# Unread products on the array, alternating input and weights, and key norms moved into the next block: two layers of a hybrid encoder on one Trainium2 core

## The chip, the core and the metric

The kernel runs on one core of a Trainium2 (trn2) chip. The metric is device time in microseconds (us) of one execution of the program; lower is better. The program is one launch that reads all its inputs and weights from HBM and writes the result there.

## What is computed

Two layers of an encoder trunk over x of 256 positions by 1024 features, in float32 throughout. Cut to what matters here:

```python
def reference(x, mem, ...):
    h = x
    for l in range(2):
        hn = rms_norm(h, norm_mix[l])
        if l == 0:
            z = hn @ hy_w_in                          # 1024 x (1824 RWKV columns + 512 S5 columns)
            y_a = rwkv7_time_mix(z[..., :1824], ...)  # 8 heads of 64, a recurrence over time
            y_b = s5_ssm(z[..., 1824:], ...)          # diagonal complex scan, 32 groups
            y_mix = concatenate([y_a, y_b]) @ hy_w_out
        else:
            y_mix = diff_attention(hn, ...)
        h = h + y_mix
        h = h + memory_cross_attention(rms_norm(h, norm_xattn[l]), rms_norm(mem, norm_mem[l]), ...)
        hn = rms_norm(h, norm_ffn[l])
        y_ff = swiglu(hn, ...) if l == 0 else moe_swiglu(hn, ...)   # 8 experts, top 2
        h = h + y_ff
    return h

def memory_cross_attention(h, mem_n, w_q, w_kv, q_gain, k_gain, w_o):
    k, v = split(mem_n @ w_kv, 2)                     # 256 x 1024 each
    k = rms_norm(k.reshape(1, 256, 4, 256), k_gain)   # a norm per head
    ...
```

The memory keys and values depend on `mem` and on the weights alone, not on h, so they can be computed at any time before the attention that reads them.

## The kernel before, in words

**Products.** Activations stand feature-major, in 8 blocks of 128 features by 256 positions. A float32 matrix product is done in three products of a reduced type: each operand is split in a high part (`xh`, `wh`) and a rest (`xl`, `wl`), and `mm3` (L188 to L192) issues high by high, high by rest, rest by high. The generator `chunks` (L164) loads two blocks of weights (512 KB) by a DMA on SP into a `raw` buffer (L173), lets ACT make `wh` by a copy (L178) and DVE `wl` by a subtraction (L184). `weight_pools(cx, raw, split, per)` sets how many raw and split buffers there are; in the stages of layer 0 in question `(3, 2, 2)`: three raw buffers.

**Start.** The input x (1 MB) is loaded in four DMAs on SP (L251), then the constants (L252); ACT and DVE split it in `xh` (L257) and `xl` (L258). `first_factor` (L261 to L280) squares x on ACT (L265), adds on POOL (L267), sums over features on the array, takes the power −1/2 and spreads the norm's factor over the partitions by a product with a diagonal matrix (`dg`, L278) into `rsB0`. The u-projection (the 512 S5 columns) runs through `feat_linear` meanwhile, in PSUM tiles `pm`, and `uT` (L300) is its result times `rsB0`. Then come the other input columns, first those of `hy_m`.

**Chain and filler.** The RWKV recurrence and the S5 scan of layer 0 are a long chain of small array products (32x32 and 32-row ones: `pbu`, `py`, `pm<-w,aa`, `pm<-qq,vt`) with DVE, POOL and ACT between. Beside them the kernel computes the memory keys and values of both layers, `memory_kv(l)` (L478 to L516), as filler for the array: four blocks n per layer (n = 0, 1 keys, n = 2, 3 values), each two PSUM tiles `pf` of 128 x 512, accumulated over 8 blocks of weights split by ACT and DVE (`fwh` L450, `fwl` L453). The function is a generator: every `yield` gives a cost and returns to a pipeline that puts pieces of chain and of filler in turn, and a scheduler then sets the order on every engine.

After a key block the norm stands between it and the next block: ACT squares `pf` straight from PSUM (L499), POOL makes the power −1/2 (`rsqrt_small`, L200 and L201), ACT scales from PSUM into `kx` (L504), the array transposes `kx` (`ptf`, L508, in a tile of the same PSUM pool as `pf`), ACT multiplies by the gain (L512), and a DMA on POOL's queue stores it (L515).

```python
            for b in range(2):
                kx = fs2.tile([128, 512], F32, name="kx", tag="kx")
                if n >= 2:
                    nc.scalar.activation(kx, p[b], AF.Copy)
                    nc.gpsimd.dma_start(vdr[l][2 * b + n - 2], kx)
```

**Router.** In front of the experts of layer 1 the array makes the logits (`lgp`) and transposes the tokens (`pt`, L1646); then `choose()` takes the two largest on DVE (L1688 to L1694, the last writes `sel`), and the array's next work is the ranks `rkp` from `sel`. After it the experts' products (`pgt`, `pgu`, `pd`) read 352 MB of weights; SP loads each MB as a buffer comes free (L1808).

Of the kernel before, what the change touches and what calls it, by code (L numbers as in the profile page):

```python
# [18 lines left out]
EPS = 1e-6  # L19
# [37 lines left out]
KX = 1  # L57
# [66 lines left out]
def kernel(ctx: ExitStack, tc: tile.TileContext, a: dict, out: bass.AP, dbg=None):  # L124
# [104 lines left out]
    fs2 = scoped(cright, "fs2", 2, side="right")  # L229
# [20 lines left out]
    for c in range(0, 8, X0C):  # L250
        nc.sync.dma_start(x0[:, c:c + X0C], a["xT"][:, c:c + X0C])  # L251
    nc.sync.dma_start(cst, a["consts"])  # L252
    one = sp.tile([128, 128], F32, name="one")
    nc.gpsimd.memset(one, 1.0)
    for c in range(8):
        g = col("gn0", c)
        nc.scalar.activation(xt[0][:, c], x0[:, c], AF.Copy, scale=g)  # L257
        nc.vector.scalar_tensor_tensor(xt[1][:, c], x0[:, c], g, xt[0][:, c], op0=ALU.mult, op1=ALU.subtract)  # L258
# [24 lines left out]
    first_factor()  # L283
# [14 lines left out]
    feat_linear(a["hy"][3], [(p[m // 2][:, m % 2], m * 128, 128, m % 2 == 0) for m in range(4)])  # L298
# [178 lines left out]
    def memory_kv(l):  # L477
# [3 lines left out]
        nc.gpsimd.tensor_tensor(gg, cols[:, lo:hi], cols[:, lo2:hi2], op=ALU.mult)  # L481
        for n in range(4):
            p = [ps_fl.tile([128, 512], F32, name="pf", tag="fl") for b in range(2)]
            for k, wh, wl in fchunks(a["wkv"][4 * l + n], 8, f"gm{l}"):
                for b in range(2):
                    t = slice(b * 128, (b + 1) * 128)
                    mm3(p[b], (mth[:, k, t], mtl[:, k, t]), (wh, wl), k == 0, k == 7)
                    yield 0.65
            for b in range(2):
                kx = fs2.tile([128, 512], F32, name="kx", tag="kx")  # L490
                if n >= 2:
                    nc.scalar.activation(kx, p[b], AF.Copy)
                    nc.gpsimd.dma_start(vdr[l][2 * b + n - 2], kx)
                    yield 0.0
                    continue
                ss = smf.tile([128, 2], F32, name="ssk", tag="ss2")
                for j in range(2):
                    js = slice(j * 256, j * 256 + 256)
                    nc.scalar.activation(kx[:, js], p[b][:, js], AF.Square, accum_out=ss[:, j:j + 1])  # L499
                rs = smf.tile([128, 2], F32, name="rsk", tag="ss2")  # L500
                rsqrt_small(rs, ss, 2, 1.0 / 256, EPS, smf)
                for j in range(2):
                    js = slice(j * 256, j * 256 + 256)
                    nc.scalar.activation(kx[:, js], p[b][:, js], AF.Copy, scale=rs[:, j:j + 1])  # L504
                yield 0.0
                pt = ps_fl.tile([128, 2, 2, 128], F32, name="ptf", tag="fl")
                for c in range(4):
# [1711 lines left out]
```

## Time and profile before

| what | value |
|---|---|
| median of 3 runs | 1676.42 us (1673.38 to 1678.52) |
| the profiled execution: its time | 1677.01 us |
| the profiled execution: span of the trace | 1675.1 us |
| PE (TensorE) busy | 1606.2 us, 96% |
| DVE (VectorE), ACT (ScalarE), POOL (GpSimd) busy | 645.6, 480.1, 207.4 us |
| mean granted clock of TensorE | 0.975 |

The profiled execution's time is 1.9 us longer than its span, and 0.6 us above the median. Busy time counts instructions that run; PE is the matmuls, PEld the weight loads that go beside them. The granted clock is given as a share of full speed; a stretch shows either 1.00 (2.4 GHz) or 0.50 (1.2 GHz). "Idle before <- releaser" says how long an engine stood in front of an instruction, and whose work ended that.

### The profile page before, as it was taken

The numbers are of one execution on the slowest core, as the hardware profiler recorded it, in microseconds if no ns is written. First come the engines' busy times: TensorE is split into PE (matmuls) and PEld (weight loads), VectorE is DVE, ScalarE is ACT, GpSimd is POOL, SyncE is SP. The second block draws the span as 40 slices with busy tenths as digits, with TensorE's granted clock in tenths as the row PEclk, the third lists the DMA queues.
The fourth block names the chain that finished last, engine by engine and source line by source line (L and its number), as shares of the span: only waits on it lengthen the run. The fifth ranks groups of instructions, "written<-read, shape, count | busy, mean of one in ns | idle before, by whom it ended". The sixth has DMA issues, their size and how long they took to land. (4 is left out here: it accounts for less than half of the span.)

```text
span 1675.1 us, 34301 instructions
## 1 busy us (share of the span) xinstructions
PE 1606.2 (96%) x14830; PEld 977.4 (58%) x14830; DVE 645.6 (39%) x1081; ACT 480.1 (29%) x861; POOL 207.4 (12%) x256
## 2 busy tenths in 40 slices
PE   5999999999999999998999999999999899999997
PEld 5867657899999988898324333343333323333432
DVE  7778987676555567764201011100101001011011
ACT  6465434554544456653101000010000100010000
POOL 6334473121000032111000000000000000000000
PEclk9999979999999999999899999999999999999998
DMA  6423323564555543645789889999999999999895
GB/s 224 153 89 126 105 75 113 221 257 150 181 195 173 187 147 127 251 139 201 301 354 399 335 363 405 404 419 418 418 419 418 419 419 418 418 419 392 346 419 238
DMA packets 74464, 471.50 MB, mean 281 GB/s; under 512 B 8600, under 2 KB 10008, under 8 KB 22464
## 3 DMA queue, kind: packets, MB, share of 16 engines
q1 hardware_dynamic: 73024, 465.02, 71.5%
q0 software_dynamic: 1280, 4.20, 0.7%
q8 instruction: 118, 1.93, 0.5%
q14 instruction: 42, 0.34, 0.1%
HBM read 463.94 MB, written 5.24 MB: 280 GB/s over the span
## 5 line engine op out<-in xcount | busy, mean ns | idle before, releaser
L195 PE MATMUL pgu<-raw,gx 128*32 128x512 f32 (+1 forms) x5376 | 520.5, 544 | 5.7 <-DMA raw<-mg 3.3
L195 PEld LDWEIGHTS pgu<-raw,gx 128*32 128x32 f32 x5376 | 171.4, 111 | 330.8 <-issue 290.0
L195 PE MATMUL pd<-raw,th 128*32 128x512 f32 x2352 | 262.7, 597 | 0.4 <-DVE th L1908 0.4
L184 DVE TENSOR_TENSOR wl<-raw,wh 128x1024 fp32r<-128x1024 f32 (+1 forms) x159 | 194.0, 1232 | 105.2 <-ACT wh L178 104.9
L178 ACT ACTIVATE wh<-raw 128x1024 fp32r<-128x1024 f32 (+1 forms) x160 | 165.6, 1047 | 149.2 <-PE pgu L191 69.2
L1894 DVE SCALAR_TENSOR_TENSOR actA<-pgu,gs,actA 128x512 f32<-128x512 f32 (+1 forms) x32 | 21.9, 684 | 481.2 <-ACT actA L1890 272.6
L195 PEld LDWEIGHTS pd<-raw,th 128*32 128x32 f32 x2352 | 76.4, 111 | 174.9 <-issue 171.8
L190 PE MATMUL pm<-xh,wh 128*128 128x256 f32 (+1 forms) x552 | 161.1, 295 | 15.2 <-ACT wh L178 13.3
L192 PE MATMUL pm<-xh,wl 128*128 128x256 f32 (+1 forms) x552 | 157.9, 290 | 5.3 <-DVE wl L184 5.3
L191 PE MATMUL pm<-xl,wh 128*128 128x256 f32 (+1 forms) x552 | 158.6, 289 | 2.1 <-DVE xl L1096 2.1
L1890 ACT ACTIVATE actA<-pgu,gs 128x512 f32<-128x512 f32 (+1 forms) x32 | 20.3, 635 | 444.8 <-PE pgu L195 444.7
L190 PEld LDWEIGHTS pm<-xh,wh 128*128 128x128 f32 (+1 forms) x552 | 106.7, 194 | 18.4 <-ACT wh L178 13.8
L192 PEld LDWEIGHTS pm<-xh,wl 128*128 128x128 f32 (+1 forms) x552 | 106.1, 194 | 7.4 <-DVE wl L184 6.6
L191 PEld LDWEIGHTS pm<-xl,wh 128*128 128x128 f32 (+1 forms) x552 | 107.1, 194 | 3.6 <-DVE xl L1096 2.5
L191 PE MATMUL pgu<-xl,wh 128*128 128x256 f32 x352 | 99.3, 282 | 0.0
L190 PE MATMUL pgu<-xh,wh 128*128 128x256 f32 x352 | 99.2, 282 | 0.0
L192 PE MATMUL pgu<-xh,wl 128*128 128x256 f32 x352 | 99.1, 282 | 0.0
L1833 POOL CAST mv<-cst 128x256 fp32r<-128x256 f32 x8 | 3.6, 448 | 650.9 <-PE ptp L195 626.0
L192 PEld LDWEIGHTS pgu<-xh,wl 128*128 128x128 f32 x352 | 66.4, 189 | 0.0
L191 PEld LDWEIGHTS pgu<-xl,wh 128*128 128x128 f32 x352 | 66.3, 188 | 0.0
L190 PEld LDWEIGHTS pgu<-xh,wh 128*128 128x128 f32 x352 | 66.2, 188 | 0.0
L453 DVE SCALAR_TENSOR_TENSOR fwl<-fraw,cols,fwh 128x512 fp32r<-128x512 f32 x64 | 56.1, 885 | 11.6 <-ACT fwh L450 11.6
(482 smaller groups left out, 2182.3 us busy)
## 6 DMA issues: line engine op xcount, KB each, us to landing
raw<-mg SPq DMA_DIRECT2D x112, 1024.0 KB, 19.1
raw<-mu SPq DMA_DIRECT2D x112, 1024.0 KB, 17.9
raw<-md SPq DMA_DIRECT2D x112, 1024.0 KB, 18.7
raw<-wgu SPq DMA_DIRECT2D x22, 1024.0 KB, 4.9
fraw<-wkv SPq DMA_DIRECT2D x32, 512.0 KB, 3.8
raw<-wqkv SPq DMA_DIRECT2D x12, 1024.0 KB, 4.9
raw<-wdn SPq DMA_DIRECT2D x11, 1024.0 KB, 4.8
raw<-hy SPq DMA_DIRECT2D x16, 512.0 KB, 3.9
```

The source lines that it names most:

```text
L178: W["act"].append(nc.scalar.activation(wh, rv, AF.Copy).ins)
L184: W["dve"].append(e_.tensor_tensor(wl[:, c_], rv[:, c_], wh[:, c_], op=ALU.subtract).ins)
L190: nc.tensor.matmul(out, lhsT=lt[0], rhs=r[0], start=start, stop=False, **kw)
L191: nc.tensor.matmul(out, lhsT=lt[0], rhs=r[1], start=False, stop=False, **kw)
L192: nc.tensor.matmul(out, lhsT=lt[1], rhs=r[0], start=False, stop=stop, **kw)
L195: nc.tensor.matmul(out, lhsT=lt, rhs=r, start=start, stop=stop, **kw)
L453: e_.scalar_tensor_tensor(wl, rv, g, wh, op0=ALU.mult, op1=ALU.subtract)
L1833: nc.gpsimd.tensor_copy(mv[:, :, 0:128], ident[:, None, :].to_broadcast([128, 2, 128]))
L1890: nc.scalar.activation(actA, p[0], AF.Silu, scale=gs[:, 0, 1:2])
L1894: nc.vector.scalar_tensor_tensor(actA, p[1], gs[:, 0, 1:2], actA, op0=ALU.mult, op1=ALU.mult)
```

## The change

Five edits:

1. `awake(p, n, x)` issues n products of a 128x128 float32 tile with itself into a PSUM tile that nothing reads. 24 stand at the very start (of the tile `one`, all ones), 12 after the router's logits and tokens (of the identity).
2. `entry()` loads x in four pairs of blocks and alternates each pair with the u-projection's weight loads on SP, and the splits likewise on ACT and DVE; the constants are loaded, and `first_factor` issued, after the u-projection's products.
3. In `memory_kv` each block is copied from PSUM to `kx` by one ACT operation. The key norm is a generator of its own, `keys()`, which works from SBUF, puts its transposes in the PSUM pool `ps_tr`, and is run after k = 2 and k = 4 of the next block's products.
4. The pool `fs2`, which holds `kx` and `kx2`, has three buffers instead of two.
5. The `weight_pools` of the stage that reads `w_glu` and `hy_out` has two raw buffers instead of three.

```diff
--- before.py
+++ after.py
@@ -226,7 +226,7 @@
     fkp = scoped(cright, "fkp", 1, side="right")
     frw = scoped(cright, "frw", 2, side="right")
     fwp = scoped(cright, "fwp", 3, side="right")
-    fs2 = scoped(cright, "fs2", 2, side="right")
+    fs2 = scoped(cright, "fs2", 3, side="right")
     smf = scoped(cright, "smf", 2, side="right")
     cx = ExitStack()
     s5t = scoped(cx, "s5t", 2)
@@ -247,15 +247,15 @@
     x0 = sp.tile([128, 8, T], F32, name="x0")
     nc.sync.dma_start(cols, a["cols"])
     xt = new_xt(xtp1)
-    for c in range(0, 8, X0C):
-        nc.sync.dma_start(x0[:, c:c + X0C], a["xT"][:, c:c + X0C])
-    nc.sync.dma_start(cst, a["consts"])
     one = sp.tile([128, 128], F32, name="one")
     nc.gpsimd.memset(one, 1.0)
-    for c in range(8):
-        g = col("gn0", c)
-        nc.scalar.activation(xt[0][:, c], x0[:, c], AF.Copy, scale=g)
-        nc.vector.scalar_tensor_tensor(xt[1][:, c], x0[:, c], g, xt[0][:, c], op0=ALU.mult, op1=ALU.subtract)
+
+    def awake(p, n, x):
+
+        for _ in range(n):
+            nc.tensor.matmul(p[:, 0:128], lhsT=x, rhs=x, start=True, stop=True, skip_group_check=True)
+
+    awake(ps_fl.tile([128, 128], F32, name="awake", tag="fl"), 24, one)
     rsB0 = rp.tile([128, T], F32, name="rsB0")
 
     def first_factor():
@@ -280,7 +280,7 @@
         nc.scalar.activation(rsB0, p, AF.Copy)
 
     gts, gstt, gtt = nc.gpsimd.tensor_scalar, nc.vector.scalar_tensor_tensor, nc.gpsimd.tensor_tensor
-    first_factor()
+
     def feat_linear(src, groups, cw=512):
 
         for k, wh, wl in chunks(src, 8, cw):
@@ -295,7 +295,28 @@
     yb = uT
 
     p = [ps_mm.tile([128, 2, T], F32, name="pm", tag="mm") for _ in range(2)]
-    feat_linear(a["hy"][3], [(p[m // 2][:, m % 2], m * 128, 128, m % 2 == 0) for m in range(4)])
+
+    def entry():
+
+        for c in range(0, 8, 2):
+            nc.sync.dma_start(x0[:, c:c + 2], a["xT"][:, c:c + 2])
+            for e in (c, c + 1):
+                g = col("gn0", e)
+                nc.scalar.activation(xt[0][:, e], x0[:, e], AF.Copy, scale=g)
+                nc.vector.scalar_tensor_tensor(xt[1][:, e], x0[:, e], g, xt[0][:, e], op0=ALU.mult, op1=ALU.subtract)
+            yield
+
+    pairs, w8 = entry(), chunks(a["hy"][3], 8, 512)
+    for k in range(8):
+        if k % 2 == 0:
+            next(pairs)
+        _, wh, wl = next(w8)
+        for m in range(4):
+            ms = slice(m * 128, m * 128 + 128)
+            mm3(p[m // 2][:, m % 2], (wh[:, ms], wl[:, ms]), (xt[0][:, k], xt[1][:, k]),
+                k == 0 and m % 2 == 0, k == 7, skip_group_check=True)
+    nc.sync.dma_start(cst, a["consts"])
+    first_factor()
     for m2 in range(2):
         nc.vector.tensor_tensor(uT[:, 2 * m2:2 * m2 + 2], p[m2], rsb(2), op=ALU.mult)
     hcst = hk.tile([128, NHCONST], F32, name="hcst")
@@ -479,6 +500,7 @@
         lo, hi = COLS[f"gq{l}"]
         lo2, hi2 = COLS[f"gk{l}"]
         nc.gpsimd.tensor_tensor(gg, cols[:, lo:hi], cols[:, lo2:hi2], op=ALU.mult)
+        late = []
         for n in range(4):
             p = [ps_fl.tile([128, 512], F32, name="pf", tag="fl") for b in range(2)]
             for k, wh, wl in fchunks(a["wkv"][4 * l + n], 8, f"gm{l}"):
@@ -486,34 +508,36 @@
                     t = slice(b * 128, (b + 1) * 128)
                     mm3(p[b], (mth[:, k, t], mtl[:, k, t]), (wh, wl), k == 0, k == 7)
                     yield 0.65
+                if k in (2, 4) and late:
+                    yield from late.pop(0)
             for b in range(2):
                 kx = fs2.tile([128, 512], F32, name="kx", tag="kx")
+                nc.scalar.activation(kx, p[b], AF.Copy)
                 if n >= 2:
-                    nc.scalar.activation(kx, p[b], AF.Copy)
                     nc.gpsimd.dma_start(vdr[l][2 * b + n - 2], kx)
-                    yield 0.0
-                    continue
-                ss = smf.tile([128, 2], F32, name="ssk", tag="ss2")
-                for j in range(2):
-                    js = slice(j * 256, j * 256 + 256)
-                    nc.scalar.activation(kx[:, js], p[b][:, js], AF.Square, accum_out=ss[:, j:j + 1])
-                rs = smf.tile([128, 2], F32, name="rsk", tag="ss2")
-                rsqrt_small(rs, ss, 2, 1.0 / 256, EPS, smf)
-                for j in range(2):
-                    js = slice(j * 256, j * 256 + 256)
-                    nc.scalar.activation(kx[:, js], p[b][:, js], AF.Copy, scale=rs[:, j:j + 1])
+                else:
+                    late.append(keys(l, gg, n, b, kx))
                 yield 0.0
-                pt = ps_fl.tile([128, 2, 2, 128], F32, name="ptf", tag="fl")
-                for c in range(4):
-                    nc.tensor.transpose(pt[:, c // 2, c % 2], kx[:, c * 128:(c + 1) * 128], ident)
-                kx2 = fs2.tile([128, 2, 2, 128], F32, name="kx2", tag="kx")
-                for e in range(2):
-                    if KX:
-                        nc.scalar.activation(kx2[:, :, e], pt[:, :, e], AF.Copy, scale=gg[:, e:e + 1])
-                    else:
-                        nc.vector.tensor_scalar(kx2[:, :, e], pt[:, :, e], gg[:, e:e + 1], None, op0=ALU.mult)
-                nc.gpsimd.dma_start(kdr[l][2 * n + b], kx2.rearrange("p a b c -> p (a b c)"))
-                yield 0.45
+
+    def keys(l, gg, n, b, kx):
+
+        ss = smf.tile([128, 2], F32, name="ssk", tag="ss2")
+        kx2 = fs2.tile([128, 2, 2, 128], F32, name="kx2", tag="kx")
+        for j in range(2):
+            nc.scalar.activation(kx2[:, j].rearrange(f2), kx[:, j * 256:j * 256 + 256], AF.Square, accum_out=ss[:, j:j + 1])
+        rs = smf.tile([128, 2], F32, name="rsk", tag="ss2")
+        rsqrt_small(rs, ss, 2, 1.0 / 256, EPS, smf)
+        for j in range(2):
+            js = slice(j * 256, j * 256 + 256)
+            nc.scalar.activation(kx[:, js], kx[:, js], AF.Copy, scale=rs[:, j:j + 1])
+        yield 0.0
+        pt = ps_tr.tile([128, 2, 2, 128], F32, name="ptf", tag="tr")
+        for c in range(4):
+            nc.tensor.transpose(pt[:, c // 2, c % 2], kx[:, c * 128:(c + 1) * 128], ident)
+        for e in range(2):
+            nc.scalar.activation(kx2[:, :, e], pt[:, :, e], AF.Copy, scale=gg[:, e:e + 1])
+        nc.gpsimd.dma_start(kdr[l][2 * n + b], kx2.rearrange("p a b c -> p (a b c)"))
+        yield 0.45
 
     low_priority(lambda: behind(MAT, memory_norm), LPM)
     cs_.close()
@@ -752,7 +776,7 @@
     ps_bm = scoped(cx, "ps_bm", 3, space=PSUM)
     ps_po = scoped(cx, "ps_po", 1, space=PSUM)
     ub = scoped(cx, "ub", 2)
-    weight_pools(cx, 3, 2, 2)
+    weight_pools(cx, 2, 2, 2)
     rs2 = scoped(cx, "rs2", 2)
     u1 = scoped(cx, "u1", 1)
 
@@ -1719,6 +1743,7 @@
                 tokens(j - 2)
         for f in TORD:
             (logits if f > 0 else tokens)(abs(f))
+        awake(ps_mm.tile([128, 128], F32, name="awake", tag="mm"), 12, ident)
     hv = hT.rearrange("p (j b) t -> p b j t", b=2)
 
     choose()
```

The new order on each engine, at three places. First ACT at the start, before the change (`x_122` is the input, `ac`, `sq` its squares, `s5t`, `s5c`, `tbl` the S5 tables):

```order
L257 ACT_TABLE_LOAD
L257 ACTIVATE xh<-x_122,cols 128x256 x2
L265 ACTIVATE ac_150<-x_122 128x512
L257 ACTIVATE xh<-x_122,cols 128x256 x2
L265 ACTIVATE sq_151<-x_122 128x512
L257 ACTIVATE xh<-x_122,cols 128x256 x4
L265 ACTIVATE sq_151<-x_122 128x512
L178 ACTIVATE wh<-raw 128x1024 x2
```

and with it:

```order
L305 ACT_TABLE_LOAD
L305 ACTIVATE xh<-x_122,cols 128x256 x2
L265 ACTIVATE ac_298<-x_122 128x512
L178 ACTIVATE wh<-raw 128x1024
L305 ACTIVATE xh<-x_122,cols 128x256 x2
L265 ACTIVATE sq_299<-x_122 128x512
L178 ACTIVATE wh<-raw 128x1024
L355 ACTIVATE s5t_335<-cols 128x16
L305 ACTIVATE xh<-x_122,cols 128x256 x2
L265 ACTIVATE sq_299<-x_122 128x512
```

The first weight split moves from behind all eight splits of x and three squares to behind two splits and one square.

PE in the recurrence of layer 0, where the keys of layer 1's block n = 0 are normed, before:

```order
L195 MATMUL pbu<-uT,sbw 128x256 x2
L195 MATMUL pm<-w,aa 32x32 x17
L195 MATMUL py<-xc,cpad 32x256
L195 MATMUL pm<-w,aa 32x32 x20
L195 MATMUL py<-xc,cpad 32x256
L195 MATMUL pm<-w,aa 32x32 x27
L195 MATMUL pm<-qq,vt 32x32 x21
L508 MATMUL ptf<-cst,kx 128x128 x4
L195 MATMUL pm<-qq,vt 32x32 x11
```

and with the change, at the same block's transposes:

```order
L190 MATMUL pf<-fwh,mth 128x512
L191 MATMUL pf<-fwl,mth 128x512
L192 MATMUL pf<-fwh,mtl 128x512
L195 MATMUL pm<-qq,vt 32x32
L190 MATMUL pf<-fwh,mth 128x512
L195 MATMUL pm<-qq,vt 32x32 x4
L536 MATMUL ptf<-cst,kx 128x128 x4
L195 MATMUL pm<-qq,vt 32x32 x27
L191 MATMUL pf<-fwl,mth 128x512
L192 MATMUL pf<-fwh,mtl 128x512
```

No `pf` product stood between the small products before; now those of the next block do, and the transposes stand among them.

PE at the router, before:

```order
L195 MATMUL lgp<-ones,sqr 128x1 x4
L1646 MATMUL pt<-cst,hT 128x128 x4
L195 MATMUL rkp<-sel,mcst 128x16
L195 MATMUL rkp<-sel,ones 128x8
```

and with the change:

```order
L1670 MATMUL pt<-cst,hT 128x128 x4
L256 MATMUL awake<-cst 128x128 x12
L195 MATMUL rkp<-sel,mcst 128x16
L195 MATMUL rkp<-sel,ones 128x8
```

The twelve unread products stand where the array waited for `sel`.

## Rows read from the trace of the kernel before

**Rows 1.** Cores: span and mean granted clock.
```profile
core 0: 1675.1 us, clock 0.975
```

**Rows 2.** Windows: stretch, us; busy of PE, PEld, DVE, ACT, POOL; clock; DMA; GB/s.
```profile
0.00:36.60 36.60, 18.72 (x116) 17.71 (x117) 25.01 (x60) 25.76 (x46) 24.13 (x48) 0.91 0.70 230
...
225.60:242.70 17.10, 16.71 (x291) 10.28 (x292) 15.38 (x25) 6.54 (x17) 13.44 (x17) 0.50 0.06 20
...
263.10:300.00 36.90, 36.90 (x266) 29.68 (x265) 22.98 (x46) 17.42 (x37) 8.45 (x12) 1.00 0.41 140
```

**Rows 3.** Waits of PE, 0 to 42 us: total, times, longest.
```profile
PE pm L190 <- ACT wh L178: 13.3, 2, 11.7
```

**Rows 4.** Timeline of PE: start, length, what, [idle before <- releaser].
```profile
11.73 0.58 PE L190 MATMUL pm<-xh,wh 128*128 128x256 f32 x1 [11.73 <-ACT wh L178]
...
17.41 0.28 PE L190 MATMUL pm<-xh,wh 128*128 128x256 f32 x1
```

**Rows 5.** Timeline of ACT at the start.
```profile
5.87 0.91 ACT L257 ACTIVATE xh<-x,cols 128x256 fp32r<-128x256 f32 x2
...
10.64 2.10 ACT L178 ACTIVATE wh<-raw 128x1024 fp32r<-128x1024 f32 x2
...
18.93 3.30 ACT L412 ACTIVATE tbl<-cst,s5c 128x256 f32<-128x256 f32 x8 [4.92 <-POOL s5c L345]
...
33.41 0.36 ACT L280 ACTIVATE rsB<-ssp 128x256 f32<-128x256 f32 x1
```

**Rows 6.** Timeline of DVE: the result of the u-projection.
```profile
35.62 1.28 DVE L300 TENSOR_TENSOR uT<-pm,rsB 128x512 f32<-128x512 f32 x2
```

**Rows 7.** Timeline of PE in the recurrence, around the key norm.
```profile
219.72 1.26 PE L195 MATMUL pm<-qq,vt 32*32 32x32 f32 x122
...
223.44 1.13 PE L195 MATMUL pbu<-uT,sbw 32*128 32x256 f32 x4 [0.88 <-DVE zz L562]
...
225.99 1.06 PE L195 MATMUL py<-xc,cpad 128*32 128x256 f32 x2 [1.00 <-POOL xc L575]
...
228.66 0.91 PE L195 MATMUL pm<-w,aa 32*32 32x32 f32 x51
...
230.10 1.11 PE L508 MATMUL ptf<-cst,kx 128*128 128x128 f32 x4
...
238.82 0.78 PE L190 MATMUL pf<-fwh,mth 128*128 128x512 f32 x1
```

**Rows 8.** Timeline of ACT, that norm: first square, scaling.
```profile
221.91 0.39 ACT L499 ACTIVATE kx<-pf 128x256 f32<-128x256 f32 x1 [3.70 <-PE pf L192]
...
228.81 0.84 ACT L504 ACTIVATE kx<-pf,rsk 128x256 f32<-128x256 f32 x2 [5.46 <-POOL rsk L201]
```

**Rows 9.** Timeline of PE at the router.
```profile
790.24 1.09 PE L1646 MATMUL pt<-cst,hT 128*128 128x128 f32 x4
795.69 0.61 PE L195 MATMUL rkp<-sel,mcst 128*128 128x16 f32 x2 [4.35 <-DVE sel L1694]
```

**Rows 10.** Windows at the router and after it, columns as in rows 2.
```profile
795.70:802.45 6.75, 6.75 (x32) 4.26 (x36) 5.92 (x41) 0.71 (x3) 0.41 (x2) 0.50 0.83 311
...
802.50:1088.00 285.50, 278.36 (x2698) 99.00 (x2694) 30.54 (x60) 25.25 (x52) 2.21 (x9) 0.99 0.92 367
```

**Rows 11.** Timeline of ACT: the split that reads the second load of hy_out.
```profile
322.81 1.06 ACT L178 ACTIVATE wh<-raw 128x1024 fp32r<-128x1024 f32 x1 [1.78 <-PE pf L191]
```

**Rows 12.** Timeline of ACT, the norm of layer 0's first key block.
```profile
87.81 0.39 ACT L499 ACTIVATE kx<-pf 128x256 f32<-128x256 f32 x1
...
89.75 0.84 ACT L504 ACTIVATE kx<-pf,rsk 128x256 f32<-128x256 f32 x2
```

**Rows 13.** Timeline of POOL: one form of addition at two places.
```profile
29.68 2.56 POOL L471 TENSOR_TENSOR ss<-ss,ssb 128x1 f32<-128x1 f32 x1
...
42.83 0.37 POOL L471 TENSOR_TENSOR ss<-ss,ssb 128x1 f32<-128x1 f32 x1
```

**Rows 14.** Waits of SP's queue, 690 to 1100 us: total, times, longest.
```profile
SPq L1808 <- PE pgu L195: 167.5, 50, 14.8
```

## The prediction

> **What bounds the kernel now.** I began with the clock. The mean granted clock is 0.975 [rows 1]; a stretch shows 1.00 or 0.50, so some 5% of 1675 us, about 84 us, ran at the lower level, and had all of it been bound by the array, some 42 us would be lost there. That is the most that this change's clock work can draw on, and each place has to be found.
>
> Then the stages, in windows [rows 2, 10]. From 263 to 300 us the array is busy all the time at full clock: there the time is the array's work. From 802.5 to 1088 us it is busy 278.36 of 285.5 us; SP's queue stands 167.5 us for buffers that `pgu` must give back [rows 14], so the weights follow the array there, and work that starts earlier should end earlier. Two places are different. In the first 36.6 us the array is busy only 18.72 us. And from 225.6 to 242.7 us it is busy 16.71 of 17.10 us, but at clock 0.50 throughout.
>
> For the first place I read PE's waits: 13.3 us for ACT's weight split, 11.7 of them in front of the first product [rows 3, 4]. The reader should see that the first product is not what ends the stage, though. Products come until after 31 us, and `uT`, the result that the next columns' PSUM tiles wait for, is made at 35.62 us [rows 6], behind `rsB` at 33.41 on ACT [rows 5]. ACT's list up to `rsB` is the path to follow.
>
> For the second place I read PE's timeline [rows 7]: 32x32 products, `pbu`, `py` and two sets of transposes, no `pf` until 238.82 us. At full clock 122 records of 32x32 took 1.26 us, in the stretch 51 took 0.91: per record about 10 against 18 ns. The clock was full again 3.9 us after `pf` had come back.
>
> **The change part by part, against the profiled 1677.0 us.**
>
> *Start (unread products, alternating loads, consts and first_factor later).* In ACT's new order the first weight split stands behind two splits of x and one square instead of eight and three. The first product could start near 8.3 us instead of 11.73: 5.87 plus 0.91 for two splits, plus a square (about 0.6), plus half of 2.10 for one weight split [rows 5]. But the 24 unread products stand ahead on the array. Four 128x128 records at half clock took 1.09 us [rows 9], with their overlap about 0.22 us apart; a float32 product makes two records, so 48 records take 10.5 us at half clock from about 1 us on: they end at 11.5 if the clock never rises, near 9 if it rises on the way. So I expect the first product at 8.5 to 11.5. In exchange the real products run at full clock, which before began at 17.41 us [rows 4]. What decides is ACT up to `rsB`. Before, ACT idled 4.92 us in front of `tbl` for a value of POOL's [rows 5], which starts from an ACT operation that now comes some 1.6 us earlier; two pairs of x splits, a weight split and squares (about 4 us) now fill that wait. I count: `tbl` from about 17.3 to 20.6, table load and two small ones to 22.2, fourth split, then as before three `fwh`, two squares, three table operations and two small splits (8.8 us with the fourth split), so `rsB` at about 31.3 and `uT` at 31.5 instead of 35.62, as DVE no longer puts the normed memory ahead of it. That is 4.1 us, and 0.4 more for a clock already full: **−4.5 us**. On SP's queue x's last pair, and the constants behind it, now stand behind three weight loads; in the first 36.6 us DMA has 0.70 of its share [rows 2], and `tbl`, the first reader of the constants, isn't due before 17 us, so I cost that at nothing. Bounds: −9 (`tbl` does not wait at all, products follow the weights), −2 (only ACT's earlier start counts, and the unread products run to 11.5).
>
> *Keys.* The norm's array work is the same 8 sets of four transposes. What is added: one copy per key block half on ACT, about 0.6 us as for other 128x512 forms, 8 of them; ACT is busy 6.54 of 17.10 us in the stretch [rows 2], so it is covered. What moves: `pf` of the next block no longer waits behind the norm, since the copy frees the PSUM tile at once, so it stands between the small products. In the stretch the work of 16.71 us at half clock is 8.35 us at full: **−8.3 us**; the stalls of 0.88 and 1.00 us [rows 7] get work to cover them: **−1.9 us**. `pf` itself isn't less: what is taken here is not there to fill at the tail, but the tail is bound by the array [rows 2], so it shortens there by as much. The store of the keys, on POOL's queue, comes later by the same half block, and nothing in this stage reads it. Bounds: 0 (clock as before, stalls reappear) and −17 (the stalls and dips of the earlier key blocks, some 7 us, go too). For new short stalls, as chain results now stand behind pieces of filler, I put **+2 us**.
>
> The clock's rule deserves a weighing. The row shows an array busy 98% of the stretch and held at half clock. The Trainium skill, TensorE: Matmul & The Clock Gate, Part 1 (What's actually happening), says that the throttled state is the default and activity releases it. By that sentence alone a busy array needs no other work beside it, and the keys' term would be −1.9 in place of −10.2. By the rows what was done mattered: the clock stayed low through 13 us of narrow products and rose after `pf` was back [rows 7], so I take −8.3.
>
> *Router.* PE waited 4.35 us for `sel` [rows 9]. Twelve unread products are 24 records, 5.3 us at half clock, starting when the transposes end (about 791.1): they end at 796.4, 0.7 us after `rkp` started before, or at 794 if the clock rises on the way, covered. After `rkp` the array was busy 6.75 us of 6.75 at clock 0.50 [rows 10]: at full clock 3.4 us less. DVE has its own work in these 6 us, so not all comes through: **−2.5 us**; bounds −3.4 and +0.7.
>
> *Two raw buffers.* The second load of `hy_out` is read at 322.81, with ACT waiting for the array, not for the load [rows 11]; the third load moves behind it. **0**, bounds 0 and +4 (one load with its split). The third `fs2` buffer: 0, it only covers the longer life of `kx`.
>
> Sum: −4.5 − 8.3 − 1.9 + 2 − 2.5 = −15.2, so 1661.8 by the profiled execution; that one stood 0.6 us above the median of the runs: **1661 us**.
>
> **Rivals.**
>
> *A, slower: the transposes wait for POOL.* The norm goes ACT, POOL, ACT, array. In the undisturbed place it takes 2.8 us from first square to end of scaling [rows 12], in the recurrence 7.7 us [rows 8], as POOL's list there is full of S5 work. Before, PE did not stand at `ptf`, since the chain lay ahead of it. If each of 8 sets stops PE for 3 us: −17.2 (the other terms) + 24, so 1683. It cancels the gain from a mean of 2.2 us, and is slower by more than can be told from 2.8 us per set. For it: POOL is busy 13.44 of 17.10 us [rows 2], one form of addition took 2.56 us at one place and 0.37 at another [rows 13]. Against: five groups of `pf` stand between scaling and transposes in the new order. The Trainium skill, SBUF — State Buffer, Who interferes with whom, says a VectorE instruction with two SBUF inputs blocks a GpSimd one that reads SBUF; the two additions agree with such a block, no run here shows that it is one. Chance 0.08.
>
> *B: the clock still falls.* The filler comes too thin among small products, or the low stretch moves elsewhere in the recurrence. Without −8.3 the sum is −6.9: 1669.5. For it: 32x32 products are still most of the records there. Chance 0.12.
>
> *C: the unread products do nothing.* If they don't raise the clock, the change doesn't do there what it says: start −3.5, router +0.7, so 1677.0 − 11.0 − 0.6 = 1665. For it: the clock was low at 795.7 although the router's products had just run [rows 10]. Chance 0.07.
>
> *D: the experts' weights set the end.* Then all gain is given back while waiting for DMA, and the time stays 1676. For it: DMA is at 0.92 of its share in 802 to 1088 us [rows 10]. Against: SP waits for the array there [rows 14], and 367 GB/s can rise a little. Chance 0.05.
>
> **How the numbers follow.** The forecast has 0.68. About 0.3%, 5 us, can be told from no change: below 1671.4 is faster, above 1681.4 slower. Faster: forecast 0.68, C 0.07, B 0.12, less 0.07 for their upper tails: 0.80. Same: D and those tails, 0.12. Slower: A, 0.08. The range goes from the forecast with start and keys near their low ends (−29: 1648) to B with its start at −2 (1673). What is left out is A, D and thin tails, near 0.17.
>
> **What would show it.** Right: first product before 11.5 us with starts 0.12 us apart, `uT` near 31; `pf` between 32x32 products in the stretch around layer 1's first key block and clock 1.00 there; no PE wait in front of `ptf`; clock 1.00 by 799 at the router; expert stage as long as before, moved as a whole. Wrong: PE waits of 2 us and more at `ptf` released by ACT; a half-clock stretch over 10 us in 170 to 320 us; waits for `raw<-hy_out`; the experts' stage longer by what was won.

## The result, and the profile after

The change made the kernel **slower**: 1694.66 us median (1691.33 to 1695.01) against 1674.9 us for the kernel before, measured beside it; ratio 1.0113, 95% interval 1.0093 to 1.0133. The forecast was 1661 us, with a range of 1648 to 1673.

The profiled execution has a span of 1692.3 us, 17.2 more than [rows 1]. To find them, cut both traces at three results that every version makes: `zm` (end of the start, before the projections), `ar` from `r` (before the block matrices of the recurrence) and the first `xl<-hT` (layer 0's mixing is done). These are windows of the kernel before, cut there; the columns are those of [rows 2].

```profile
0.00:52.66 52.66, 32.57 (x212) 28.81 (x212) 40.18 (x80) 33.24 (x59) 35.27 (x63) 0.94 0.62 200
...
52.66:122.61 69.95, 66.97 (x412) 57.09 (x413) 48.01 (x69) 39.18 (x70) 19.16 (x19) 0.98 0.39 123
...
122.61:337.01 214.40, 205.41 (x2541) 151.86 (x2540) 173.23 (x275) 102.36 (x186) 90.71 (x104) 0.93 0.38 131
```

The same windows with the change:

```profile
0.00:54.16 54.16, 37.93 (x244) 35.84 (x244) 35.49 (x72) 33.16 (x59) 26.68 (x60) 0.83 0.65 214
...
54.16:145.79 91.63, 86.57 (x466) 70.53 (x466) 61.02 (x84) 48.33 (x93) 21.71 (x23) 0.89 0.29 96
...
145.79:356.10 210.31, 192.07 (x2509) 143.86 (x2509) 167.74 (x274) 97.08 (x171) 87.16 (x102) 0.94 0.40 140
```

The start is 1.5 us longer, the **projections 21.7 us longer**, the recurrence 4.1 us shorter, all the rest 1.9 us shorter (1692.3 − 356.1 against 1675.1 − 337.0). The reader should look at busy against length. In the projections the array was busy 19.6 us longer. Part of this is a lower clock: the rows have 0.89 of 91.6 us against 0.98 of 70.0 us, from which I estimate 7 to 9 us of the 19.6; the rest is work that stood elsewhere before. In the recurrence the array was busy 13.3 us less (205.41 to 192.07), and yet that part is only 4.1 us shorter: it stood idle 18.2 us instead of 9.0. Work was taken from the recurrence, where the array has waits to cover, and put into the projections, where it had stood only 3.0 us.

What that work was, grouped by operation, for PE in the projections before, and then with the change (busy us and mean ns of one, then idle before):

```profile
L190 PE MATMUL pf<-fwh,mth 128*128 128x512 f32 x32 | 12.4, 398 | 0.0
L191 PE MATMUL pf<-fwl,mth 128*128 128x512 f32 x31 | 12.3, 398 | 0.9 <-DVE fwl L453 0.9
L192 PE MATMUL pf<-fwh,mtl 128*128 128x512 f32 x31 | 12.2, 393 | 0.0
L195 PE MATMUL pm<-gup,zr 128*128 128x512 f32 (+1 forms) x8 | 4.2, 629 | 0.0
L508 PE MATMUL ptf<-cst,kx 128*128 128x128 f32 x8 | 1.3, 286 | 0.0
```

```profile
L190 PE MATMUL pf<-fwh,mth 128*128 128x512 f32 x40 | 16.4, 435 | 0.6 <-DVE mtl L212 0.6
L191 PE MATMUL pf<-fwl,mth 128*128 128x512 f32 x38 | 16.3, 428 | 1.0 <-DVE fwl L474 1.0
L192 PE MATMUL pf<-fwh,mtl 128*128 128x512 f32 x38 | 16.0, 420 | 0.0
L195 PE MATMUL pm<-gup,zr 128*128 128x512 f32 (+1 forms) x8 | 6.2, 890 | 0.0
L195 PE MATMUL pbu<-uT,sbw 32*128 32x256 f32 x12 | 3.4, 400 | 0.0
L536 PE MATMUL ptf<-cst,kx 128*128 128x128 f32 x12 | 2.8, 335 | 0.0
```

`pf` rose from 36.9 to 48.7 us (116 records instead of 94, some at half clock); S5's `pbu` (3.4 us) is new there; the transposes `ptf` rose from 1.3 to 2.8 us; `gup` costs 2.0 us more. Together 18.7 of the 19.6 us. Most of `gup` ran in a stretch at half clock:

```profile
101.00:107.80 6.80, 6.80 (x14) 3.32 (x14) 0.00 (x0) 2.75 (x8) 0.41 (x1) 0.50 0.07 27
```

The start, PE's timeline, which answers to [rows 4]:

```profile
1.05 7.72 PE L256 MATMUL awake<-one 128*128 128x128 f32 x48 [1.05 <-POOL one L251]
8.53 0.39 PE L190 MATMUL pm<-xh,wh 128*128 128x256 f32 x1
8.75 0.28 PE L191 MATMUL pm<-xl,wh 128*128 128x256 f32 x1
```

and ACT's and DVE's, which answer to [rows 5, 6]:

```profile
32.35 0.36 ACT L280 ACTIVATE rsB<-ssp 128x256 f32<-128x256 f32 x1
...
33.37 1.28 DVE L321 TENSOR_TENSOR uT<-pm,rsB 128x512 f32<-128x512 f32 x2
...
50.91 0.75 DVE L495 TENSOR_SCALAR mem<-mem,rs 128x1024 f32<-128x1024 f32 x1
...
54.16 0.68 DVE L641 TENSOR_TENSOR zm<-pm,rsB 128x512 f32<-128x512 f32 x1
```

The first product came 3.2 us earlier and `uT` 2.25 us earlier. But the normed memory now stands behind `uT` on DVE, and the transposes of its first half behind products of `hy_m` on PE; the second half, which uses the same buffer, was ready only at 50.91. PE's wait for the memory to 60 us, before:

```profile
PE pt L208 <- DVE mem L474: 1.4, 2, 0.9
```

and with the change PE's waits to 60 us, and from 60 to 345 us (answering to [rows 3]):

```profile
PE pt L208 <- DVE mem L495: 5.6, 1, 5.6
PE pm L190 <- DVE uT L321: 4.5, 1, 4.5
...
PE pm L195 <- DVE qq L847: 3.9, 3, 1.6
PE pm L195 <- DVE a L825: 3.9, 1, 3.9
PE pm L195 <- DVE w L852: 2.4, 2, 2.1
...
PE ptf L536 <- ACT kx L532: 0.6, 1, 0.6
```

5.6 us went on the memory's second half, where before both halves cost 1.4, and 4.5 on `uT`; in the recurrence PE now waits for steps of the chain (`qq`, `a`, `w`). In front of the transposes it waited 0.6 us in all. At the router, answering to [rows 9]:

```profile
808.45 1.09 PE L1670 MATMUL pt<-cst,hT 128*128 128x128 f32 x4
809.34 5.27 PE L256 MATMUL awake<-cst 128*128 128x128 f32 x24
814.45 0.29 PE L195 MATMUL rkp<-sel,mcst 128*128 128x16 f32 x2
...
816.56 0.31 PE L195 MATMUL pgt<-pf,hnh 128*128 128x96 f32 x1 [1.15 <-DVE pf L1701]
```

`rkp` starts 6.0 us after the last transposes began, against 5.45 before, and the faster products behind it run into a wait for DVE.

### The profile page after: what moved, and what is told of

Read it like the earlier page. It is cut to its first block, busy times and chain, and to the rows that moved or that the text cites. A ratio compares the mean times of both kernels' runs of the same rounds, so it can differ in the third digit from the quotient of the medians.

```text
span 1692.3 us, 34450 instructions
## 1 busy us (share of the span) xinstructions
PE 1618.4 (96%) x14902; PEld 991.6 (59%) x14902; DVE 647.6 (38%) x1081; ACT 484.3 (29%) x869; POOL 199.0 (12%) x256
## 5 line engine op out<-in xcount | busy, mean ns | idle before, releaser
L192 PE MATMUL pm<-xh,wl 128*128 128x256 f32 x552 | 157.6, 290 | 6.5 <-DVE wl L184 6.5
L192 PEld LDWEIGHTS pm<-xh,wl 128*128 128x128 f32 x552 | 106.0, 194 | 8.1 <-DVE wl L184 7.5
```

The source lines that it names most:

```text
L192: nc.tensor.matmul(out, lhsT=lt[1], rhs=r[0], start=False, stop=stop, **kw)
```

## The experiments

All ratios are to the kernel before, measured beside each.

**1. The keys alone** (edits 3, 4 and 5; the third `fs2` buffer has room only with edit 5).

> Only the key part of the change (norm moved into the next block, transposes in ps_tr, three fs2 buffers, two raw buffers for hy_out, without which the third fs2 buffer has no room). Theory T, the ring: tiles of the pool ps_tr are handed out in the order in which the program asks for them; the moved transposes ask before the S5 scan's first pbu, so S5's first groups can start only after layer 0's first key block is transposed. Then the first xc<-pbu stands near 115 us instead of 39.8 and this kernel holds nearly all of the loss: 1687 to 1696 us. Rival X, the start: the loss comes from the unread products and the alternating loads; then this kernel is at 1665 to 1678 us, whatever the place of pbu. Rival P, the norm's chain over POOL: also 1687 to 1696, but with PE waits of 2 us and more in front of ptf.

1684.97 us, ratio 1.0071 (1.0057 to 1.0084), 2 us below the range of theories T and P and 7 us above that of X. The first `xc<-pbu` stands at 104.9 us, as the ring would have it, and the only wait of PE at `ptf` is 0.6 us, so rival P is out. Its three windows, cut as above:

```profile
0.00:47.38 47.38, 29.03 (x190) 27.64 (x191) 31.85 (x70) 31.21 (x57) 30.61 (x60) 0.93 0.67 220
...
47.38:133.82 86.44, 81.49 (x480) 67.53 (x478) 62.86 (x86) 49.66 (x95) 21.68 (x23) 0.96 0.35 115
...
133.82:347.00 213.18, 195.43 (x2502) 145.12 (x2502) 168.19 (x274) 97.36 (x172) 87.18 (x102) 0.94 0.40 138
```

The same pattern as the whole change: projections 16.5 us longer, 10 us less to do in the recurrence, which is only 1.2 us shorter. In the projections `pf` took 45.2 us (116 records) instead of 36.9 (94), and S5's `pbu`, which had been in the start, 3.4 us.

**2. The same, transposes in another pool.**

```diff
-        pt = ps_tr.tile([128, 2, 2, 128], F32, name="ptf", tag="tr")
+        pt = ps_bm.tile([128, 2, 2, 128], F32, name="ptf", tag="bm")
```

> As the key part alone, with one word changed: the transposes' tile comes from the pool ps_bm instead of ps_tr. Theory T: S5's first xc<-pbu is back near 40 us and the loss is gone: 1664 to 1677 us, at least 10 us below the key part alone. Rivals X and P: the pool does not matter, within 4 us of the key part alone.

1700.97 us, ratio 1.0153 (1.0136 to 1.0169). S5's first group was back at 40.2 us, and the kernel was 16 us slower still. **Theory T's forecast failed.** `zm` came at 53.15, `ar` at 132.34, `xl<-hT` at 364.79: the projections were 9.2 us longer than before, the recurrence 18 us. This version does not tell what S5's late groups cost in experiment 1, though, as it has a new wait of its own, which was 1.2 us before. PE's waits from 100 to 160 us:

```profile
PE pb L195 <- POOL rkp L741: 10.8, 1, 10.8
```

Its projections have 96 records of `pf`, two more than before, and 105 stand ahead of the block matrices, as before: hardly any filler left the recurrence, and yet it is the slowest version.

**3. The alternating loads alone** (edit 2).

> Only the alternating loads and the later constants and first_factor, no unread products. Theory T: no loss here; uT at 32 to 34 us instead of 35.6 and 1670 to 1676 us. Rival X: 1680 to 1690 us.

1690.39 us, ratio 1.0097 (1.0081 to 1.0112): theory T's 1670 to 1676 is out, and the time lies 0.4 us above rival X's range, so this edit costs by itself, beside the keys. `uT` was at 33.3 us as forecast. `zm` came 4.3 us late (PE waited 7.2 us for the second half of `mem`), the projections took as long as before, and the recurrence 12.5 us longer:

```profile
126.58:353.50 226.92, 206.98 (x2545) 153.60 (x2545) 172.21 (x276) 101.47 (x184) 88.28 (x104) 0.93 0.37 130
```

19.9 us idle against 9.0, with nearly the same work and no edit there. The longest of PE's waits in this window is at the transposes, in a version whose key norm is that of the kernel before:

```profile
PE ptf L521 <- ACT kx L517: 5.2, 2, 4.7
```

The order on the engines is set by a planner from times that it assumes; moved by a few us at the start, it had put the recurrence in another order.

**4. The unread products of the start alone** (24 of edit 1).

> Only the 24 unread products at the start. Theory T: the real products start at the same time as before (11.7 us, ACT's split), at full clock; what ends the stage is rsB on ACT, so 1673 to 1677 us. Rival X: 1680 to 1690 us.

1673.31 us, ratio 0.9993 (0.9984 to 1.0002). No change, as expected.

**5. and 6. The keys of one layer alone.** The old norm is kept for the other layer; for layer 1 alone, cut:

```diff
             for b in range(2):
                 kx = fs2.tile([128, 512], F32, name="kx", tag="kx")
+                if n < 2 and l == 0:
...
+                    yield 0.45
+                    continue
                 nc.scalar.activation(kx, p[b], AF.Copy)
```

> The key part for layer 1's keys alone; layer 0's keys are normed as before (both raw buffers and fs2 as in the change). The first theory, the ring of ps_tr, fell with the pool's experiment. Theory F, filler spent early: freeing the PSUM tile at once lets the planner issue the next block's products where the array has no hole (between the projections), and the recurrence has too little of them later; 78 instead of 48 pf sets of one stand before pm<-zr,wlr in the key part's order, 158 instead of 105 before the block matrices. Here these counts are 48 and 105, as before. By F the kernel is as before up to 200 us, and the half-clock stretch of 17 us is filled: 1662 to 1671 us. Rival N: moving transposes among the small products harms the recurrence in itself: 1676 us or more.

> The key part for layer 0's keys alone; layer 1's are normed as before. The counts of early pf are those of the whole key part, 78 and 158. By F it has the whole loss or more: 1683 to 1692 us, and PE is busy without a hole from 60 to 105 us with 30 more pf triples than before. By N the loss is split, 1676 to 1681 us.

(The counts are of single `pf` products in the planned order.) Layer 1 alone: 1673.45 us, ratio 0.9992 (0.9980 to 1.0004). Layer 0 alone: 1693.22 us, ratio 1.0124 (1.0101 to 1.0146). Theory F's ranges were missed by 2.5 and 1.2 us, rival N's by 2.6 and 12 us. **The loss of the key part is layer 0's.** Layer 0's first block frees its PSUM tile while the projections run; before, the next block had to wait for the norm, and the counts show that this wait had kept filler for the recurrence. That the missing filler is what costs the time is argued from the idle time, not shown: the order of the recurrence is another one, too.

Layer 1 alone missed its forecast: it gained little where the prediction had put its largest term. The stretch around its first key block, before and with it:

```profile
208.50:242.70 34.20, 32.32 (x624) 20.36 (x623) 30.48 (x53) 13.36 (x29) 22.30 (x26) 0.70 0.23 73
```

```profile
207.57:242.00 34.43, 32.57 (x602) 21.60 (x601) 29.80 (x53) 14.50 (x24) 19.24 (x22) 0.85 0.30 93
...
121.82:334.05 212.23, 200.24 (x2511) 148.70 (x2510) 169.20 (x273) 101.26 (x185) 90.55 (x104) 0.94 0.38 129
...
315.00 0.50 PE L190 MATMUL pf<-xh,wh 128*128 128x256 f32 x2 [1.96 <-ACT xh L989]
```

The clock there rose from 0.70 to 0.85, half of what was hoped. The last product of `pf` for the memory stands at 311.53, before at 318.0; then PE stood 1.96 us for `xh`. The whole recurrence is 2.2 us shorter.

**7. The alternating loads with the memory early.** The offset puts the memory's norm 3000 places lower in the planner's priority.

```diff
-LPM = 3000
+LPM = 0
```

> The alternating loads alone, as in the experiment before, with the priority offset of the memory's norm 0 instead of 3000, so that the transposes of mem stand ahead of hy_m's products again, as before the change. Theory M: the 16 us of that experiment come from the second half of mem, for which PE stands 7.6 us, and from the order of the recurrence that the planner makes of the shifted times; with mem early the first is gone (zm near 50 to 53 us) and most of the second (the order of the recurrence is near that of before): 1670 to 1679 us. Rival: alternating the loads costs by itself (DMA, splits on DVE): 1685 us or more.

1669.36 us, ratio 0.9975 (0.9963 to 0.9986), 21 us below experiment 3 and 0.6 below the range. **Theory M held**: `zm` at 50.55, and the recurrence

```profile
119.00:330.85 211.85, 204.81 (x2542) 150.93 (x2540) 173.77 (x276) 102.62 (x186) 90.92 (x104) 0.94 0.39 135
```

is 7.0 us idle. This version is 0.25% faster than the kernel before.

**8. A control: the offset alone,** in the kernel before.

> The kernel before with the priority offset of the memory's norm 0 instead of 3000 and nothing else: a control. If the 4 us that the alternating loads gained with that offset come from the loads, this one stays within 2 us of before (1672 to 1676 us); if they come from the offset alone, it is at 1668 to 1671 us.

1669.73 us, ratio 0.9978 (0.9966 to 0.9989). The gain of experiment 7 is the offset's. Alternating the loads is worth nothing that can be measured.

**9. The router's products alone.**

> Only the twelve unread products at the router. By the trace of the change: rkp is free to start at the same time, the products end after it, and the clock stays at half for them, so the gain and the cost cancel: 1673 to 1676 us. By the prediction: 2.5 us less, 1671.5 us.

1675.98 us, ratio 1.0011 (0.9999 to 1.0024): no gain.

**10. Two raw buffers alone.**

> Only the third raw buffer of the stage of hy_out taken away. By the prediction it costs nothing: 1672 to 1676 us, the split of hy_out not waiting for a load. The rival bound was a wait for one load, 4 us: 1677 to 1679 us.

1675.85 us, ratio 1.0005 (0.9994 to 1.0015): nothing, as forecast.

**11. The change with both causes undone** (offset 0, layer 0's keys as before).

> The whole change with two things undone: the memory norm's priority offset is 0, and layer 0's keys are normed as before, at once. If theories M and F hold both, the loss of 20 us is gone: 1664 to 1676 us, and zm is made near 52 us, 105 sets of pf stand before the block matrices. If the parts harm each other in another way: 1682 us or more.

1691.63 us, ratio 1.0106 (1.0087 to 1.0125). **Not cured.** In its trace, which is of the fastest of four runs (1685.07 us), it was 2.0 us ahead of before at `ar`, so both causes were gone up to there. Then the recurrence took 13.8 us longer, with 19.4 us idle:

```profile
120.65:348.83 228.18, 208.77 (x2544) 154.13 (x2543) 175.73 (x277) 104.20 (x188) 90.00 (x104) 0.92 0.36 123
...
143.91 1.71 ACT L433 ACTIVATE tbl<-cst,s5c 128x256 f32<-128x256 f32 x4 [3.29 <-POOL zz L621]
145.52 0.57 ACT L812 ACTIVATE btk<-pt 128x512 f32<-128x512 f32 x1
...
146.14 1.12 PE L195 MATMUL pm<-ar,kt 64*64 64x128 f32 x8 [3.29 <-ACT btk L812]
```

`btk`, a step of the chain, stood on ACT behind S5's table, which waited for POOL. Before, the two stood the other way round, and a like wait of the table held up nothing of the chain:

```profile
142.85 0.62 ACT L765 ACTIVATE btk<-pt 128x512 f32<-128x512 f32 x1
...
146.27 0.91 ACT L412 ACTIVATE tbl<-cst,s5c 128x256 f32<-128x256 f32 x2 [2.46 <-POOL zz L574]
```

**12. That swap undone.**

```diff
             if j in (5, 9):
-                s5_table(2 + j // 8)
+                with tc.issue_after(TOK[-1]):
+                    s5_table(2 + j // 8)
```

> The change with both causes undone, as in the run before, and one more edit: S5's later tables may stand on ACT only behind the copy of btk, as they stood in the kernel before. Theory R, the order of the recurrence: in that run btk stood behind the table's operations, which waited 3.29 us for POOL, and the array waited 3.7 us in front of pm<-ar,kt; without the swap this wait is gone and the kernel is 3 to 8 us faster than 1691.6. Rival: the wait goes elsewhere, 1688 us or more.

1688.26 us (1682.34 to 1690.6), ratio 1.0075 (1.0053 to 1.0097), against a spread of 1685.07 to 1693.11 without the edit. The wait for `btk` was gone, and PE waited instead for `arb`:

```profile
PE pm L195 <- DVE arb L845: 3.9, 1, 3.9
```

The recurrence was no shorter (`ar` at 121.91, `xl<-hT` at 351.05). The time lies where the two forecasts meet, and the intervals of this experiment and the one before overlap; the trace has it as the rival said. One swap is not the lever.

**13. As 11, without the start's unread products.**

> The change with both causes undone and without the 24 unread products at the start. In the planned order btk then stands ahead of the table as before, and the order of the block matrices is that of before. Theory R: 1668 to 1677 us. Rival, the moved keys of layer 1 or the router's products cost: above 1682 us.

1670.9 us, ratio 0.9977 (0.9965 to 0.9989), 20.7 us below experiment 11. The recurrence has 11.4 us idle:

```profile
120.02:335.44 215.42, 204.00 (x2544) 152.93 (x2543) 172.86 (x276) 103.94 (x188) 89.92 (x104) 0.94 0.39 133
```

The products themselves cost nothing (experiment 4). Between the two versions the array's order in the recurrence differs in 1307 rows (counted as below, under "The order"); in this company the products made the planner choose another one.

**14. and 15. Another order and no other work:** `FILL_C`, the filler owed at the recurrence's start, 15 or 17 instead of 16. The number itself moves filler worth 1 in the costs that the pieces yield; the rest of the new order follows from it.

> The kernel before with FILL_C 15 instead of 16, the share of filler that is owed when the recurrence begins: no work is added or moved to another stage by hand, only the planner's order in the recurrence differs (2482 of its 1954 PE rows removed or added, as many as with the change). Theory R, that before stands at an order found by trying and that another one costs: 1679 to 1695 us. Rival: the order hardly matters, 1671 to 1677 us.

> The same with FILL_C 17. Theory R: 1679 to 1695 us; rival: 1671 to 1677 us.

1680.87 us, ratio 1.0037 (1.0023 to 1.0052), and 1680.5 us, ratio 1.0036 (1.0022 to 1.0050). Both slower, as theory R had it, at the low end. With 15, the recurrence has 15.2 us idle against 9.0:

```profile
123.56:339.34 215.78, 200.63 (x2527) 149.86 (x2526) 169.66 (x274) 98.25 (x181) 88.20 (x104) 0.93 0.37 125
```

It was busy 4.8 us less, though, so the window is only 1.4 us longer than before; the rest of the 5 us between the two spans stands 1.0 in the start and 2.7 behind the recurrence, too little each to be told from the scatter of the runs. Where this loss stands is not shown.

**16. Part of layer 1's keys on top of 7:** only its first block's norm inside the next block.

> The alternating loads with the offset 0, and of the keys only layer 1's first block normed inside the next block. Theory F: filler for the half-clock stretch without spending it early, 1660 to 1667 us, if the filler that is used there isn't missed at the end of the recurrence; if it is missed, as with all of layer 1's keys, the sum is that of the alternating loads, 1667 to 1671 us.

1678.86 us, ratio 1.0023 (1.0008 to 1.0037), 9.5 us above experiment 7 and outside both forecasts: again the recurrence.

```profile
121.02:345.48 224.46, 212.64 (x2544) 158.39 (x2543) 172.46 (x276) 102.68 (x186) 88.75 (x104) 0.89 0.39 134
```

Here it is not idle time, 11.8 us, but the clock: 0.89, where experiment 7 has 0.94, and the array is busy 7.8 us longer for nearly the same products.

**17. Offset 0 and the start's products, in the kernel before.**

> Before with the memory norm's offset 0 and the 24 unread products at the start. The block matrices stand in the order of before. Theory R: the products themselves cost nothing and gain little, 1665 to 1671 us, as the offset alone (1669.7). Rival: they cost by themselves, 1676 us or more.

1673.23 us, ratio 0.9998 (0.9984 to 1.0011), between the two forecasts: `zm` came at 58.14 us, 2.5 later than with the offset alone. Beside the offset the products are not quite free.

**18. The change with the offset 0.**

> The change with one thing undone, the memory norm's offset 0. Theory M: zm is made near 51 us instead of 54.2, and about 3 us come back; filler is still spent early (158 sets before the block matrices) and the recurrence is in another order: 1685 to 1693 us. Rival: the memory's place is the whole cause, 1675 us.

1690.24 us, ratio 1.0097 (1.0077 to 1.0117). `zm` was made at 45.44, 8.7 us earlier than in the change, and `ar` at 129.82, 16.0 us earlier; 11.6 of these were given back in the recurrence, with 25.0 us idle and at a lower clock:

```profile
129.82:351.72 221.90, 196.93 (x2461) 145.47 (x2460) 167.95 (x269) 94.15 (x167) 89.01 (x104) 0.88 0.37 127
```

The memory's place is not the whole cause. This version and experiment 11 differ in layer 0's keys alone, and are equal within their intervals: in this company, undoing these keys gained nothing.

## Why the prediction was wrong

**What bounds the kernel** was read too simply. "From 263 to 300 us the array is busy all the time" is true, and the step that rested on it, "what is taken here is not there to fill at the tail, but the tail is bound by the array [rows 2], so it shortens there by as much", **is the step that failed.** It asked only about the end of the recurrence. With the keys alone, 22 records of `pf` came forward into the projections, which became 16.5 us longer, and the recurrence, with 268 records instead of 292, was busy 10.0 us less and idle 8.8 us more, so it shortened by 1.2 us. That the norm's wait held back filler was nowhere in the sum.

**Keys: −8.3, −1.9 and +2 forecast; +11.1 measured for the keys alone** (experiment 1), and +17.6 in the whole change (21.7 − 4.1, with the memory's effects in it). The mechanism at the stretch was half right: with layer 1's keys alone the clock there rose to 0.85, and the recurrence was 2.2 us shorter, but the time was the same (0.9992). What lost was layer 0's keys, which the sum knows only as a bound ("the stalls and dips of the earlier key blocks, some 7 us, go too"), although all edits of a function run wherever it is called.

**Start: −4.5 forecast, +1.5 measured at `zm`, and +16.5 for the alternating loads alone** (experiment 3). First product at 8.53 (8.5 to 11.5 forecast), `rsB` at 32.35 (31.3; the terms add to 31.0), `uT` at 33.37 (31.5): the count of ACT's list was good to 1 to 2 us. **The second step that failed** is the half sentence "as DVE no longer puts the normed memory ahead of it": it named the move as a gain and did not ask who waits for the memory. PE stood 5.6 us for it (7.2 in experiment 3), and the planner made another order of all that follows. That "the real products run at full clock" held (0.28 us for a product at 8.75); it is worth nothing there, as experiment 4 shows.

**Router: −2.5 forecast, 0 measured** (ratio 1.0011). The products ended 0.55 us late, and the array then ran into DVE's own work, which the prediction had named. **Raw buffers: 0 and 0.**

**Rivals and signs.** A gave the right side (1683, about a third of the loss) by the wrong mechanism: PE waited 0.6 us at `ptf`. B came nearest. Its low stretch of 17.1 us was gone, but others came, among them a sign of being wrong that the prediction had named, a stretch of over 10 us at half clock in the recurrence:

```profile
186.40:196.60 10.20, 6.00 (x202) 5.80 (x204) 8.45 (x14) 1.90 (x4) 5.28 (x5) 0.50 0.17 55
```

and the projections fell to 0.89. B's price, 1669.5 us, was far off, as it let the other terms stand (with the start at −2 it adds to 1672 and not 1673). C and D did not occur: the router's first ranks ran faster, and the experts' part moved as a whole, 19.1 us later at `xl<-hT` and 17.2 at the end.

**The order.** The +2 us for "new short stalls" priced a recurrence in a new order, and is the term that was most mis-sized: by experiments 3, 11, 14 and 15 such an order cost 7 to 17 us with the array's work there the same within 5 us. The traces let the order itself be compared. I took the array's records from 20 us before `ar` to 5 us behind `xl<-hT` (some 2690), without the unread products, in order of their start, and counted rows removed and added against the kernel before:

| experiments | rows that differ | time |
|---|---|---|
| 9, 10, 17, 4, 8, 7 | 0, 12, 94, 122, 222, 280 | ratios 0.9975 to 1.0011, none slower |
| 16 | 822 | 1.0023 |
| 5, 13 | 901, 903 (158 between the two) | 0.9992, 0.9977 |
| 12, 11, 15, 3 | 1088, 1104, 1107, 1149 | 1.0036 to 1.0106, all slower |
| 6, 2, the change, 1, 14, 18 | 1647, 1698, 1995, 2022, 2052, 2060 | 1.0037 to 1.0153, all slower |

Every version with over 1000 rows is slower, and none with under 300; how much slower does not follow from the number, and those of the last row, save 14, also moved work. Where an experiment cost nothing, it had mostly kept the old order; 5 and 13 are the exception, and share the moved keys of layer 1. The prediction's range had no room for a new order.

Shown: that a planner's number which changes the order and no work moves the time by 0.37% (14, 15), that layer 0's keys carry the key part's loss (5, 6), that the memory's place carries the alternating loads' (3, 7). Argued from the traces: that filler missing in the recurrence is how layer 0's keys lose (2 loses without it), and that the order is how the start's products lose in experiment 11 (11, 13, 4). Open: which rows of the order cost, as undoing one swap moved the wait elsewhere (12); how much of the whole change's loss is filler and how much order, as undoing layer 0's keys gained nothing beside the start's products (11, 18); and why the parts' losses do not add up (11 and 16 us alone, 20 together).

## What to carry to other kernels

Treat filler as a store: before you free a buffer so that filler can run earlier, count how much of it will stand in stages where the array has no hole, and what is left for the stage that has waits to cover. Where a planner fixes the order on every engine, an edit can also draw a new order in stages that it does not touch; time edits with a control that redraws the order and changes no work, and compare the order in those stages with the order before. When a result moves ahead of another on an engine, ask who waits for the one that fell behind.

## What the runs showed that was not expected

One number, the memory norm's priority offset, gave 4.4 us by itself (ratio 0.9978), as much as any version with the change's parts. An order redrawn with no work changed cost 0.36 to 0.37%, where the whole change had been forecast to win 0.9%. And the 24 unread products, which cost nothing alone (0.9993), separated two otherwise equal versions by 20.7 us (experiments 11 and 13).
